# 16 instead of 32 tokens through fetched expert rows, a fixed VectorE order in the last stage, and a tail by column chunks

## The chip, the cores and the metric

One core of one Trainium2 chip runs the kernel. The metric is the device time of one execution in microseconds (us), the median of the runs. A profiled execution gives, beside its time, a trace of the instructions of each engine: TensorE (PE for matmuls, PEld for weight loads), VectorE (DVE), ScalarE (ACT), GpSimd (POOL) and the DMA queues of SyncE (SP), ScalarE and GpSimd.

## The reference

A decoder block on x of 256 tokens by 1024 features, all float32. First an RMSNorm, one input projection, two attention mixers of 8 heads each, gates, output projections and a residual add. Then the part that takes most of the time, an expert retrieval (PEER):

```python
qh = (x_blk @ w_q).reshape(tc, PEER_HEADS, 2, PEER_HALF)
scores = jnp.einsum('thpc,hpnc->thpn', qh, skf)           # 8 heads, 2 halves, 128 sub-keys
s_top, i_top = lax.top_k(scores, PEER_TOPK)               # 16 best of each half
cand = s_top[:, :, 0, :, None] + s_top[:, :, 1, None, :]  # 256 candidates
c_s, c_pos = lax.top_k(cand.reshape(...), PEER_TOPK)      # 16 experts per head
g = jax.nn.softmax(c_s, axis=-1)
u = expert_u[e_idx]; v = expert_v[e_idx]                  # rows out of 16384 experts
a = jax.nn.gelu(jnp.einsum('td,thkd->thk', x_blk, u), approximate=False)
out = jnp.einsum('thk,thkd->td', g * a, v)
```

The result is added to the residual and goes through a last RMSNorm.

## The kernel before, in words

The front (to about 253 us) does norms, projections and attention. What follows computes the experts densely for most tokens: the 16384 experts are 128 chunks of 128 (NB = 128).

**Stage U** (lines 628 to 690). For each chunk b a 512 KB block of expert_u is fetched by SyncE (L85, four buffers "raw"), split by ScalarE into a rounded high part whi (L106) and by VectorE or GpSimd into the rest wlo (L109), and multiplied with the tokens in 24 matmuls (mm3, L122: 16 with whi, then 8 with wlo), each on ND columns. ND is T - S = 256 - S; S = 32 tokens are left out of the dense work, so ND = 224. ScalarE takes GELU of the result into W[:, b] (L646). The buffers of whi and wlo are two each, so whi of chunk b waits until TensorE is through with whi of chunk b - 2. VectorE's instructions of the stage run in the order in which they are written (manual_schedule). Between the chunks stand steps of the top-k search, taken from a generator: each step yields a cost in us, and at each chunk the loop adds a rate to what is allowed: EARLY_RATE 2.4 until the first 128 tokens (tt = 1) are done, TOPK_RATE 1.1 after. While the early rate holds, GpSimd makes wlo; the switch comes when `scattered` is filled.

At the end of tt = 1 the gates gS and the places iS are known (L565 to L567), and GpSimd scatters the gates into a zeroed DRAM array gd with 128 indirect DMAs (L487); the 16 of a head must have landed before those of the next but one may write. For the other tile (tt = 0) the S tokens' indices and gates go to DRAM, and for the rest, P - S = 96 tokens, the gates are built into W on the chip in groups of four tokens (24 groups, g_build and g_use, L590 to L622), spread over the chunks that are left.

The program as a whole is ordered by a scheduler that runs a timeline of its own: on engines without a fixed order an instruction is placed when its inputs are ready there and the engine is free, wherever it is written; `issue_after` ties an instruction behind another one.

**Stage V** (L800 to L817). For each chunk b: fetch and split a block of expert_v, weigh two chunks of W with the gates read back from gd (fetch_weights L695 on GpSimd's queue, weigh L702), split W[:, b] into two parts xw (prepare: L707 on ScalarE, L709 on VectorE; xw has two buffers), and 16 matmuls into 8 accumulators: order 0 with v high on both parts (L720, 2 x ND = 448 columns) and order 1 with v low (L723, ND = 224 columns). The first fetch_weights waits for all of the scatter.

The 32 left-out tokens go by fetched rows: S // 16 = 2 groups, in each 16 gathers of expert_u rows and 16 of expert_v rows (L738 on GpSimd's queue, 128 rows of 4 KB each, two buffers), each followed by one VectorE instruction on 128 x 1024 (L749 dot product with the token, L761 weighted sum), 64 in all; at the end of a group 8 matmuls (L765). VectorE's order here is the scheduler's, with these instructions and xw tied behind the newest wlo.

**Tail.** The last LAST = 3 chunks are multiplied column chunk by column chunk c; as each of the 8 is complete, gather_up adds its three parts (L774, L775), finish transposes it (L783), adds it to h (L784) and takes squares for the norm on ScalarE (L786). Then the norm's scale (L828 to L835, with Ln and Exp on ScalarE) and four output pieces. The table for Ln and Exp is asked for at L755.

## Time and profile before

| | us |
|---|---|
| median of three runs | 1022.54 |
| lowest, highest | 1016.17, 1027.51 |
| the profiled execution | 1021.67 |
| its span, first to last instruction | 1019.9 |
| PE busy in the span | 952.3 |
| DVE busy | 767.4 |
| ACT busy | 564.0 |
| POOL busy | 430.4 |

The span is what the trace shows; the time is 1.8 us longer. Matmuls overlap and their ends are modelled, so a busy PE is read by how far apart matmuls start, not by its share. In rows with a line (L122) the line is that of the kernel before; in brackets stands the idle time of the engine before the instruction and what ended it.

### The profile page before, as it was taken

What the parts mean: (1) busy time and instruction counts of PE and PEld (TensorE: products, weight loads), DVE (VectorE), ACT (ScalarE), POOL (GpSimd) and SP (SyncE); (2) the same over time, 40 slices, a digit from 0 to 9 for tenths busy, and PEclk for the clock granted to TensorE, in tenths of its full rate; (3) what the DMA queues carried; (4) which work ended last, traced back from release to release, by engine and by line L of the source; (5) the groups of instructions that cost most, each with busy time, mean ns of one, the idle gap of its engine ahead of it and who ended that gap; (6) DMA issues with size and microseconds to landing.
All of it is one profiled execution on the core that took longest, in us unless ns stands there. A gap on an engine that the chain in (4) does not pass through costs nothing. (4 is left out here: it accounts for less than half of the span.)

```text
span 1019.9 us, 18735 instructions
## 1 busy us (share of the span) xinstructions
PE 952.3 (93%) x7099; PEld 903.6 (89%) x7099; DVE 767.4 (75%) x1433; ACT 564.0 (55%) x1032; POOL 430.4 (42%) x288
## 2 busy tenths in 40 slices
PE   9999999999888999999999998798998998889894
PEld 7898899799888999999999998787987888888793
DVE  6556767764899997777888886788788777778763
ACT  5564446543654567777777674444544444444445
POOL 0000000000657787787787783344444344444201
PEclk9999999999999999999999999999999999999997
DMA  7667685545456879777778677898988888988841
GB/s 238 211 211 247 192 255 179 181 143 167 153 148 168 203 192 237 178 190 197 176 187 199 172 195 235 322 324 302 353 311 303 287 304 291 307 281 305 279 158 42
DMA packets 86298, 230.16 MB, mean 226 GB/s; under 512 B 27392, under 2 KB 30272, under 8 KB 86080
## 3 DMA queue, kind: packets, MB, share of 16 engines
q1 hardware_dynamic: 53216, 183.07, 56.4%
q0 software_dynamic: 31008, 43.07, 15.9%
q10 hardware_dynamic: 1984, 2.84, 0.9%
q8 instruction: 55, 0.90, 0.3%
q14 instruction: 35, 0.29, 0.1%
HBM read 218.35 MB, written 10.58 MB: 224 GB/s over the span
## 5 line engine op out<-in xcount | busy, mean ns | idle before, releaser
L106 ACT CAST whi<-raw 128x1024 fp32r<-128x1024 f32 x327 | 343.5, 1050 | 379.7 <-PE acc L720 186.5
L109 DVE TENSOR_TENSOR wlo<-raw,whi 128x1024 fp32r<-128x1024 f32 x313 | 382.0, 1221 | 115.2 <-ACT whi L106 108.9
L122 PE MATMUL pj<-xh,whi 128*128 128x224 f32 (+1 forms) x1280 | 304.5, 279 | 5.8 <-ACT whi L106 5.8
L122 PE MATMUL pj<-xl,whi 128*128 128x224 f32 (+1 forms) x1280 | 303.8, 279 | 0.1
L720 PE MATMUL acc<-xw,whi 128*128 128x448 f32 x1024 | 237.7, 372 | 39.1 <-DVE xw L709 38.3
L487 POOL DMA_INDIRECT gd<-gS,iS x128 | 242.8, 1897 | 70.8 <-issue 35.8
L122 PEld LDWEIGHTS pj<-xh,whi 128*128 128x128 f32 x1280 | 248.2, 194 | 6.9 <-ACT whi L106 6.2
L122 PEld LDWEIGHTS pj<-xl,whi 128*128 128x128 f32 x1280 | 248.1, 194 | 0.6 <-DVE xl L182 0.4
L720 PEld LDWEIGHTS acc<-xw,whi 128*128 128x128 f32 x1024 | 182.9, 188 | 60.7 <-DVE xw L709 45.1
L122 PE MATMUL pj<-xh,wlo 128*128 128x224 f32 (+1 forms) x1280 | 175.8, 279 | 3.7 <-DVE wlo L109 3.7
L122 PEld LDWEIGHTS pj<-xh,wlo 128*128 128x128 f32 x1280 | 159.8, 193 | 5.1 <-DVE wlo L109 3.9
L109 POOL TENSOR_TENSOR wlo<-raw,whi 128x1024 fp32r<-128x1024 f32 x14 | 33.5, 2408 | 267.1 <-ACT whi L106 260.3
L723 PEld LDWEIGHTS acc<-xw,wlo 128*128 128x128 f32 x1024 | 135.4, 191 | 3.5
L723 PE MATMUL acc<-xw,wlo 128*128 128x224 f32 x1024 | 137.5, 273 | 0.0
L695 POOL DMA_DIRECT2D gq<-gd x64 | 37.0, 579 | 110.0 <-DVE W L702 57.6
L738 POOL DMA_INDIRECT rows<-in_v_dram,places x32 | 57.8, 1805 | 52.7 <-DVE sm L761 36.9
L738 POOL DMA_INDIRECT rows<-in_ur_dram,places x32 | 53.7, 1678 | 49.7 <-DVE rows L749 47.6
L707 ACT CAST xw<-W 128x224 fp32r<-128x224 f32 x128 | 47.5, 373 | 3.6 <-DVE W L702 3.4
L709 DVE TENSOR_TENSOR xw<-W,xw 128x224 fp32r<-128x224 f32 x128 | 49.3, 386 | 0.2
L749 DVE SCALAR_TENSOR_TENSOR rows<-rows,xr 128x1024 f32<-128x1024 f32 x32 | 39.0, 1221 | 10.1 <-DMA rows<-in_ur_dram,places 8.1
L646 ACT ACTIVATE W<-pj 128x224 f32<-128x224 f32 (+24 forms) x128 | 41.5, 324 | 8.4 <-PE pj L122 8.4
L761 DVE SCALAR_TENSOR_TENSOR sm<-rows,a,sm 128x1024 f32<-128x1024 f32 x30 | 38.4, 1280 | 0.4 <-DMA rows<-in_v_dram,places 0.3
(212 smaller groups left out, 967.2 us busy)
## 6 DMA issues: line engine op xcount, KB each, us to landing
raw<-in_ut_dram SPq DMA_DIRECT2D x128, 512.0 KB, 4.0
raw<-in_v_dram SPq DMA_DIRECT2D x128, 512.0 KB, 4.2
raw<-in_wf_dram SPq DMA_DIRECT2D x72, 512.0 KB, 3.9
gd<-zfill SPq DMA_DIRECT2D x16, 512.0 KB, 5.1
gq<-gd POOLq DMA_DIRECT2D x64, 128.0 KB, 4.7
gd<-gS,iS POOLq DMA_INDIRECT x128, 5.0
h<-in_x_dram SPq DMA_DIRECT2D x4, 256.0 KB, 4.8
sks<-in_skt_dram ACTq DMA_DIRECT2D x1, 1024.0 KB
```

Source lines behind the costliest of these rows:

```text
L106: last_hi = nc.scalar.copy(hi, src)
L109: last_lo = rest.tensor_sub(lo, src, hi.bitcast(F32))
L122: nc.tensor.matmul(o, a, b, start=first and i == 0, stop=last and i == len(seq) - 1)
L487: d = nc.gpsimd.indirect_dma_start(gd[:, :], bass.IndirectOffsetOnAxis(ap=iS[:, k:k + 1], axis=0), gS[:, k:k + 1], None, compute_op=ALU.add)
L646: gl = nc.scalar.activation(W[:, b, nd:ND], ps[:, nd:ND], AF.Gelu)
L707: nc.scalar.copy(w[:, 0], W[:, b])
L709: nc.vector.tensor_sub(w[:, 1], W[:, b], w[:, 0].bitcast(F32))
L720: nc.tensor.matmul(acc[c][:, S:S + 2 * ND], v_h[:, cs], w.rearrange("p a b -> p (a b)"), start=b == 0, stop=False, skip_group_check=True)
L723: nc.tensor.matmul(acc[c][:, S:S + ND], v_l[:, cs], w[:, 0], start=False, stop=b == NB - 1, skip_group_check=True)
L738: nc.gpsimd.indirect_dma_start(rows[n][:, :], None, (u_rows if kind == "u" else v_rows)[:, :], bass.IndirectOffsetOnAxis(ap=places[:, g, k ...
L749: nc.vector.scalar_tensor_tensor(r, r, 1.0, xr, op0=ALU.mult, op1=ALU.mult, accum_out=a[:, g, k:k + 1])
L761: nc.vector.scalar_tensor_tensor(sm, r, a[:, g, k:k + 1], sm, op0=ALU.mult, op1=ALU.add)
```

## The change

- S goes from 32 to 16: ND is 240, one group of fetched rows (32 gathers and VectorE products, not 64), 28 groups of gates built on the chip, not 24.
- The top-k generator: its costs and TOPK_RATE are raised; all four index casts of ScalarE are written after the first pair of the second search; Exp and the normalisation are written later; GpSimd hands wlo back to VectorE when the searches of tt = 1 end (`shared`), not when the scatter is issued.
- Stage V: VectorE in the written order (wlo, xw of the next chunk, weigh, then a fetched row's product at most once in two chunks); xw has three buffers; ScalarE's half of xw is tied behind whi.
- The table load for the norm is tied behind the last GELU.
- Tail: LAST is 2; PE, VectorE and ScalarE in the written order; squares of columns 0 to 511, 512 to 895 and the last 128 are taken in three pieces, half on VectorE; the product with the norm's gains on GpSimd comes before the norm's scale is known.

```diff
-LAST = 3
+LAST = 2
-TOPK_RATE = 1.1
+TOPK_RATE = 1.3
-S = 32
+S = 16
-    xsp = ctx.enter_context(tc.tile_pool(name="xsplit", bufs=2))
+    xsp = ctx.enter_context(tc.tile_pool(name="xsplit", bufs=3))
+            shared = ["searches"]
                         yield from best16([(sv[:, pp, k16], si[:, pp, k16], sc[tt][:, 2 * hd + pp])
-                                           for pp in range(2)], 0.205)
+                                           for pp in range(2)], 0.25)
...
-                        pp, hh = h0 // 4, 4 * (h0 // 2 % 2)
-                        nc.scalar.copy(sx[pp][:, hh:hh + 4]...)
-                        yield from best16([...], 0.14)
+                        if h0 == 2:
+                            for pp in range(2):
+                                for hh in (0, 4):
+                                    nc.scalar.copy(sx[pp][:, hh:hh + 4]...)
+                                yield 0.0
+                        yield from best16([...], 0.2)
+                    shared.clear()
+                    yield 0.0
...
-                    nc.scalar.activation(ge, ge, AF.Exp)
...
+                        if pp == 0:
+                            nc.scalar.activation(ge, ge, AF.Exp)
...
-                        nxt = load(ut[b + 1], [P, 8, P], rest=nc.vector if scattered else nc.gpsimd)
+                        nxt = load(ut[b + 1], [P, 8, P], rest=nc.gpsimd if shared else nc.vector)
...
-                        allowed += TOPK_RATE if scattered else EARLY_RATE
+                        allowed += EARLY_RATE if shared else TOPK_RATE
...
         def prepare(b):
             w = (vp if b == NB - 1 else xsp).tile([P, 2, ND], F32R, name="xw", tag="xw")
-            nc.scalar.copy(w[:, 0], W[:, b])
-            with tc.issue_after(last_lo.ins):
-                nc.vector.tensor_sub(w[:, 1], W[:, b], w[:, 0].bitcast(F32))
+            with tc.issue_after(last_hi.ins):
+                nc.scalar.copy(w[:, 0], W[:, b])
+            nc.vector.tensor_sub(w[:, 1], W[:, b], w[:, 0].bitcast(F32))
...
                         if g == ng - 1:
-                            nc.scalar.preload_act_table_set("natural_log_exp_and_others")
+                            with tc.issue_after(gl.ins):
+                                nc.scalar.preload_act_table_set("natural_log_exp_and_others")
...
+        with tc.manual_schedule(engines={mybir.EngineType.DVE}):
+            for b in range(NB):
+                v_h, v_l = load(v[b], [P, D], vp if b % 3 == (NB - 1) % 3 else splp)
+                if b == 0:
+                    weigh(0)
+                    w_next = prepare(0)
+                parts = (v_h, v_l, w_next)
+                if b + 1 < NB:
+                    w_next = prepare(b + 1)
+                if b % 2 == 0:
+                    weigh(b + 2)
+                    fetch_weights(b + 4)
...
+                if b % 2 and b >= 3:
+                    while done * (NB - 24) <= (b - 3) * 32 * ng:
+                        next(steps, None)
+                        done += 1
...
+        with tc.manual_schedule(engines={mybir.EngineType.PE, mybir.EngineType.DVE, mybir.EngineType.Activation}):
+            for c in range(4):
+                for order in range(2):
+                    products(b0, c, parts0, order)
+            for c in range(8):
+                for order in range(2):
+                    products(b1, c, parts1, order)
+                    if c < 4:
+                        products(b0, c + 4, parts0, order)
+                rests.append(gather_up(c))
+                if c:
+                    finish(c - 1, rests[c - 1])
+                if c == 5:
+                    squares_of(0, 0, 4)
+                    for tt in range(2):
+                        nc.gpsimd.tensor_mul(h[:, tt, :512], h[:, tt, :512], gf[:, :512])
+            squares_of(1, 4, 7)
+            finish(7, rests[7])
+            squares_of(2, 7, 8)
```

## Rows read from the trace of the kernel before

**Rows 1.** The head of the page.
```profile
span 1019.9 us, 18735 instructions
```

**Rows 2.** Busy time by stretches of the span: the stretch, its length, then busy us and instructions of PE, PEld, DVE, ACT, POOL, the granted clock, the DMA share, GB/s.
```profile
253.10:308.50 55.40, 48.25 (x399) 47.70 (x397) 49.71 (x227) 29.30 (x41) 33.51 (x14) 0.94 0.48 147
...
387.00:623.40 236.40, 236.40 (x2114) 236.40 (x2112) 186.79 (x259) 172.91 (x416) 181.93 (x98) 1.00 0.78 193
626.60:645.00 18.40, 16.09 (x96) 14.59 (x96) 10.82 (x17) 8.55 (x14) 4.87 (x10) 1.00 0.95 336
645.00:977.00 332.00, 298.22 (x1826) 276.01 (x1825) 260.95 (x380) 151.73 (x230) 142.47 (x119) 1.00 0.87 301
```

**Rows 3.** Matmuls of TensorE in order of time (start us, us, line): the first and the last of 16 that follow one another on 256 columns, and of 16 on 224 columns.
```profile
230.18 0.28 PE L122 MATMUL pj<-uh,whi 128*128 128x256 f32 x1
...
231.96 0.28 PE L122 MATMUL pj<-ul,whi 128*128 128x256 f32 x1
...
598.38 0.28 PE L122 MATMUL pj<-xh,whi 128*128 128x224 f32 x1
...
600.06 0.27 PE L122 MATMUL pj<-xl,whi 128*128 128x224 f32 x1
```

**Rows 4.** The chain of work that ended last, in stage V (start us, us until the next piece, what).
```profile
961.40 1.91 PE acc L720 x8
...
966.00 1.19 DVE sm L761
967.55 1.91 PE acc L720 x8
...
975.37 1.70 PE acc L765 x16
...
982.20 1.63 PE acc L720 x8
983.83 0.88 PE acc L723 x8
```

**Rows 5.** One row of the view of waits: who waited, for whom, us in all, times, longest.
```profile
PE acc L720 <- DVE xw L709: 38.3, 48, 3.0
```

**Rows 6.** Groups of VectorE's instructions by line over the whole span (line, operation, out<-in, shapes, count | busy us, mean ns | idle before).
```profile
L109 DVE TENSOR_TENSOR wlo<-raw,whi 128x1024 fp32r<-128x1024 f32 x313 | 382.0, 1221 | 115.2 <-ACT whi L106 108.9 <-PE pj L241 2.4 <-PE pj L122 2.1
L709 DVE TENSOR_TENSOR xw<-W,xw 128x224 fp32r<-128x224 f32 x128 | 49.3, 386 | 0.2
L749 DVE SCALAR_TENSOR_TENSOR rows<-rows,xr 128x1024 f32<-128x1024 f32 x32 | 39.0, 1221 | 10.1 <-DMA rows<-in_ur_dram,places 8.1 <-DMA xr<-xd 2.0
L702 DVE TENSOR_TENSOR W<-W,gq 128x256 f32<-128x256 f32 x64 | 26.8, 419 | 4.4 <-DMA gq<-gd 4.4
```

**Rows 7.** From the scatter to stage V, in order of time: VectorE's places iS, GpSimd's first scatter and the first read of gd, TensorE's first product of V.
```profile
307.92 0.29 DVE L567 TENSOR_SCALAR iS<-W,pcol 128x128 uint32<-128x128 f32 x1
308.50 1.79 POOL L487 DMA_INDIRECT gd<-gS,iS  x1 [6.11 <-DVE W L472]
619.88 1.17 POOL L695 DMA_DIRECT2D gq<-gd  x2 [3.94 <-DMA gd<-gS,iS]
626.62 1.65 PE L720 MATMUL acc<-xw,whi 128*128 128x448 f32 x7 [3.02 <-DVE xw L709]
```

**Rows 8.** The three gaps of TensorE early in stage U, and ScalarE's instructions at two of them; the first row is ScalarE's at the start of the kernel.
```profile
2.03 1.28 ACT L755 ACT_TABLE_LOAD   x1
269.68 1.99 ACT L528 CAST W<-W 128x1024 bf16<-128x1024 uint32 x2 [4.90 <-DVE W L474]
272.91 0.37 PE L122 MATMUL pj<-xh,whi 128*128 128x224 f32 x1 [3.02 <-ACT whi L106]
289.79 0.31 ACT L534 ACTIVATE W<-W 128x128 f32<-128x128 f32 x1 [2.71 <-DVE W L533]
292.75 0.37 PE L122 MATMUL pj<-xh,whi 128*128 128x224 f32 x1 [2.77 <-ACT whi L106]
310.82 2.05 PE L122 MATMUL pj<-xh,wlo 128*128 128x224 f32 x8 [3.68 <-DVE wlo L109]
```

**Rows 9.** VectorE in the last steps of tt = 1: the start of the first step after the searches, and the same product twice, the first while GpSimd made a wlo.
```profile
288.89 0.86 DVE L533 TENSOR_TENSOR W<-W 128x128 f32<-128x128 f32 x1
292.81 3.42 DVE L556 TENSOR_TENSOR W<-W 128x2048 bf16<-128x2048 bf16 x1
304.36 1.22 DVE L556 TENSOR_TENSOR W<-W 128x2048 bf16<-128x2048 bf16 x1
```

**Rows 10.** The tail in order of time: the first and the last product, one pair of transposes, the two table loads, the first of the last products on VectorE.
```profile
994.61 0.38 PE L720 MATMUL acc<-xw,whi 128*128 128x448 f32 x1
1002.39 0.35 PE L723 MATMUL acc<-xw,wlo 128*128 128x224 f32 x1
1004.05 0.44 PE L783 MATMUL tpv<-ident,rest 128*128 128x128 f32 x2 [0.56 <-DVE rest L775]
1010.06 1.28 ACT L830 ACT_TABLE_LOAD   x1
1011.58 1.28 ACT L831 ACT_TABLE_LOAD   x1
1013.90 1.41 DVE L843 SCALAR_TENSOR_TENSOR o<-h,st,gf 128x512 f32<-128x512 f32 x2
```

**Rows 11.** DMA issues: out<-in, queue, operation, count, median us from issue to landing.
```profile
rows<-in_ur_dram,places POOLq DMA_INDIRECT x32, 6.3
```

More of the change, by code (lines that the diff above doesn't have):

```diff
@@ L759, in fetched_steps @@
                 else:
-                    with tc.issue_after(last_lo.ins):
-                        nc.vector.scalar_tensor_tensor(sm, r, a[:, g, k:k + 1], sm, op0=ALU.mult, op1=ALU.add)
+                    nc.vector.scalar_tensor_tensor(sm, r, a[:, g, k:k + 1], sm, op0=ALU.mult, op1=ALU.add)
                 yield
@@ L793, in block_kernel @@
         fetch_weights(2)
-        weigh(0)
-        w_next = prepare(0)
-        for b in range(NB):
-            w = w_next
-            parts = (*load(v[b], [P, D], vp if b % 3 == (NB - 1) % 3 else splp), w)
-            if b < NB - LAST:
-                for order in range(2):
-                    for c in (range(8) if b else (4, 5, 6, 7, 0, 1, 2, 3)):
-                        products(b, c, parts, order)
-            else:
-                kept.append((b, parts))
-            if b + 1 < NB:
-                w_next = prepare(b + 1)
-            if b % 2 == 0:
-                weigh(b + 2)
-                fetch_weights(b + 4)
-            if b == 3:
-                nc.scalar.dma_start(gf, gf_row.partition_broadcast(P))
-                nc.scalar.dma_start(sel, consts[:, 1153:1153 + GS])
-            if b >= 1:
-                while done * (NB - 12) <= (b - 1) * 64:
-                    next(steps, None)
-                    done += 1
@@ L817, in block_kernel @@
-        rests = []
-        for c in range(8):
-            for b, parts in kept:
-                for order in range(2):
-                    products(b, c, parts, order)
-            rests.append(gather_up(c))
-            if c > 1:
-                finish(c - 2, rests[c - 2])
-        finish(6, rests[6])
-        finish(7, rests[7])
-        ss, r, t = st[:, 20:22], st[:, 22:24], st[:, 24:26]
-        nc.vector.tensor_reduce(ss, sq, AX.X, ALU.add)
-        nc.vector.tensor_scalar(ss, ss, 1.0 / D, EPS, op0=ALU.mult, op1=ALU.add)
@@ L830, in block_kernel @@
[L830 to L844 removed]
+        with tc.manual_schedule(engines={mybir.EngineType.DVE}):
[10 more added lines that the diff above has]
+                    fetch_weights(b + 4)
+                if b == 3:
+                    nc.scalar.dma_start(gf, gf_row.partition_broadcast(P))
+                    nc.scalar.dma_start(sel, consts[:, 1153:1153 + GS])
+                if b < NB - LAST:
+                    for order in range(2):
+                        for c in (range(8) if b else (4, 5, 6, 7, 0, 1, 2, 3)):
+                            products(b, c, parts, order)
+                else:
+                    kept.append((b, parts))
+                if b % 2 and b >= 3:
+                    while done * (NB - 24) <= (b - 3) * 32 * ng:
+                        next(steps, None)
+                        done += 1
@@ new lines, in block_kernel @@
+        rests = []
+        ss, r, t = st[:, 20:22], st[:, 22:24], st[:, 24:26]
+        (b0, parts0), (b1, parts1) = kept
+        with tc.manual_schedule(engines={mybir.EngineType.PE, mybir.EngineType.DVE, mybir.EngineType.Activation}):
+            for c in range(4):
+                for order in range(2):
+                    products(b0, c, parts0, order)
+            for c in range(8):
+                for order in range(2):
+                    products(b1, c, parts1, order)
[11 more added lines that the diff above has]
+            squares_of(2, 7, 8)
+            nc.vector.tensor_reduce(ss, sq, AX.X, ALU.add)
+            nc.vector.tensor_scalar(ss, ss, 1.0 / D, EPS, op0=ALU.mult, op1=ALU.add)
+            nc.scalar.activation(r, ss, AF.Ln)
+            nc.scalar.activation(r, r, AF.Exp, scale=-0.5)
+            nc.vector.tensor_mul(t, r, r)
+            nc.vector.tensor_mul(t, t, ss)
+            nc.vector.tensor_scalar(t, t, -0.5, 1.5, op0=ALU.mult, op1=ALU.add)
+            nc.vector.tensor_mul(r, r, t)
+            for tt in range(2):
+                o = rawp.tile([P, D], F32, name="o", tag="raw")
+                rt = r[:, tt:tt + 1]
+                nc.scalar.activation(o[:, :512], h[:, tt, :512], AF.Copy, scale=rt)
+                nc.vector.scalar_tensor_tensor(o[:, 512:], h[:, tt, 512:], rt, gf[:, 512:], op0=ALU.mult, op1=ALU.mult)
+                nc.scalar.dma_start(out[tt][:, :512], o[:, :512])
+                nc.sync.dma_start(out[tt][:, 512:], o[:, 512:])
```

59 lines of the change are left out of this document (23 added, 36 removed).

## The prediction

> **What bounds the kernel now.** I read the stretches first, then the order of time at their seams, the chain of waits, and the groups of instructions.
>
> The span is 1019.9 us [rows 1]. The front, to 253.1, is the same code before and after, so I keep it. Stage U lasts to 623.3. From 387 on TensorE is without a gap: 2114 matmuls in 236.4 us, 0.112 us each; at its start it is not: 399 in 55.4 us, at a granted clock of 0.94 [rows 2]. Three gaps stand there, 3.02, 2.77 and 3.68 us [rows 8]. 128 chunks of 24 matmuls at 0.1115 us are 342.5 us, the 24 groups 24 x 4 x 0.119 = 11.4; 370.2 us passed, so U loses 16.3.
>
> The first product of V stands at 626.62, and what released it is not the end of U. VectorE makes iS at 307.92, the first scatter goes at 308.50, and the first read of gd goes at 619.88, ended by the scatter's landing [rows 7]. From iS to V's first product 318.7 us pass on GpSimd's queue, whatever TensorE does meanwhile. U ended 3 us earlier by coincidence.
>
> In V a chunk that waits for nothing takes 1.63 + 0.88 = 2.51 us; where a fetched row's product stands in the chain, two chunks take 6.15 us (961.40 to 967.55) instead of 5.02 [rows 4]. TensorE waited 38.3 us for xw [rows 5]. VectorE has, per chunk, wlo 1.22, xw 0.39, half of a weighing 0.21, and 64 fetched products of 1.22 to 1.28 over 116 chunks, 0.69: together 2.51, all of a chunk [rows 6]. With two xw buffers, xw of the next chunk starts only when TensorE is through with the last one, and any long instruction ahead of it becomes a gap. Loss in all: the last three chunks start at 994.61 [rows 10]; with one of them counted in, 126 chunks took 997.1 - 626.6 = 370.5 us, against 316.3 + 3.4 for the two groups' small matmuls, so V loses 50.8 us.
>
> **The change part by part.**
>
> *Columns.* ND = 240 is 7% more for TensorE, but that isn't what the spacing says. 16 columns take 1.70/16 = 0.106 us each, 224 columns 0.110 in V [rows 4] and 0.112 in U (15 steps in 1.68 us), 256 columns 0.1187 [rows 3], 448 columns 0.2038. Below some 235 columns something other than columns sets the spacing; above, the line from 256 to 448 has 0.000443 us per column. It gives 0.1116 at 240 and 0.2180 at 480. I take 0.1125 for 240, just over the floor; bounds are 0.110 and 0.1153 (halfway between 224 and 256). The cost in U is 24 x 0.001 x 128 = 3.1 us (bounds -5 to 12); four more groups are 1.9. A chunk of V becomes 8 x (0.2180 + 0.1125) = 2.644 us, so 126 chunks are 333.1 instead of 316.3: +16.8 (+14 to +20).
>
> The Trainium skill, "TensorE: Matmul & The Clock Gate", section "Back-to-back issue gap", gives a gap of N/2.4 + 2.5 ns; by it alone each 240-column matmul costs 6.7 ns more than a 224-column one. The same page's "LDWEIGHTS" has a weight load at columns/1.2, 107 ns for 128, which is the floor that the 16-column matmuls show. The sum goes by the floor; a price in columns is rival 2.
>
> *Top-k and the scatter.* The searches of tt = 1 are the same instructions and end at 288.89 [rows 9]. From there to iS took 19.0 us. In it four instructions were stretched while GpSimd made a wlo: L556 took 3.42 beside it and 1.22 alone [rows 9]; with three short ones that were held in the same way (the first, L533, took 0.86) the excess adds up to 7.1, so the steps alone are 12. After the change GpSimd makes no wlo in this stretch, but VectorE makes those of chunks 14 to 21: by the new costs the searches end in chunk 12 (29.0 at 2.4 each) and iS comes in chunk 20 (12.5 more at 1.3). 288.9 + 12 + 8 x 1.13 = 310.0. TensorE can be later: wlo of chunk 21 waits for whi, that for chunk 19's high products, 253.1 + 19 x 2.70 + 1.8 = 306.2, then 1.05, 1.2 and 0.8: 309.3 plus whatever TensorE has lost by then.
>
> Does it still lose the first two gaps? The change writes ScalarE's casts and Exp later in the program. But ScalarE isn't in written order here: a table load written in V (L755) ran at 2.03, and the casts that waited 4.90 us ran four chunks before the chunk that they were written in [rows 8]. Their inputs don't change, so I lean to the gaps staying. They cost 3.02 + 2.77 and about 3.3 of half clock behind them (matmuls 0.21 apart), 9.1. So iS is at 310.0 to 318.4, and V starts 318.7 later, at 628.7 to 637.1; I take the middle, 633 (+6.4). The third gap, wlo queued behind steps on VectorE, goes, since the steps are now handed out 1.3 us a chunk. But U's end no longer matters: 253.1 + 345.6 + 13.3 + some 7 is 619, and TensorE then idles some 14 us for the scatter.
>
> VectorE in the group part of U becomes fuller: 28 groups of about 3.3 us over 75 chunks, 93 + 75 x 1.31 = 191 of 216 us, where it had 187 of 236 [rows 2]. ScalarE's waits inside a group could then reach TensorE; up to 9 us of that is hidden by the idle time before V. The cover fails at 11.
>
> A fuller VectorE could also slow the scatters. They take 1.55 at best and 1.88 on average while VectorE is 79% busy; if the excess went with its busy time, 128 x 0.33 x 0.13 = 6 us. The Trainium skill, "SBUF — State Buffer", section "Who interferes with whom", says that GpSimd can't write descriptors while VectorE holds the shared ports in its two-port modes, which products of two tensors don't have. By that rule the added work, all such products, costs the scatters nothing. No run here separates the two; 0 stands in the sum and 6 in the range.
>
> *Stage V.* VectorE has 1.22 + 0.41 + 0.21 + 32 x 1.25 over 104 chunks, 0.38: 2.22 of 2.644 us. xw is written ahead of the fetched product, and with a third buffer it may be made two chunks ahead, so a 1.25 us instruction behind it has more than a chunk of cover. ScalarE's half of xw goes behind whi, one chunk earlier than needed. A gather is asked for two steps, over six chunks or 16 us, before its product; it lands in 6.3 us [rows 11]. What stays is the start: six chunks in 18.4 us [rows 2], 3.3 lost, 1.7 of half clock after the idle time (as behind the gap at 272.91), and 2 for the rest: 7 of the 50.8. Bounds are 3 and 25, half of today's. The DMA share was 0.87 with 0.55 fetched rows (280 KB) per chunk beside 576 KB; with 0.31 rows and a shorter chunk the rate is (576 + 158)/2.644 = 278 GB/s, below the 301 that it ran at [rows 2]. One group's eight small matmuls are 0.9.
>
> *Tail.* From the end of the 126th chunk to the end of the span it was 1019.9 - 997.1 = 22.8. After: 1.3 us for four products of the last but one chunk; then TensorE's written order, in which transposes of c - 1 wait behind products of c for ScalarE's copy and VectorE's add, some 1.2 us after the product. Stepping through the eight, with pairs of transposes of 0.44 [rows 10], the last ends 8.5 later. Then add 0.6, squares of 128 columns 0.5, the scale 1.3 instead of 3.84 since both table loads (1.28 each) go when the load is tied behind the GELU, and 6.0 from the first output product to the end as now [rows 10]: 18.2 (bounds 16.5 to 20.5).
>
> **The sum.** 633 + 333.1 + 0.9 + 7 + 18.2 = 992.2 of span, 27.7 less. The profiled time stands 1.8 above its span, and the median 0.9 above the profiled execution: 995.
>
> **The rivals.**
>
> 1. *VectorE still holds V.* The fixed order makes it stand at one instruction while another is ready, so half of the loss stays, 25 us. For it: 84% busy leaves little. Against: the third buffer. 995 + 18 = 1013.
> 2. *Columns cost in proportion.* 0.1195 for 240. U: 367 + 13.3 + 9 puts its end at 642.6, past the scatter; V starts at 646 and its chunk is 2.69: 646 + 338.9 + 0.9 + 7 + 18.6 + 2.7 = 1014. Against it are 16 to 224 columns at one spacing [rows 3, 4].
> 3. *The group part of U is VectorE's.* If its end slips by over 11 us, V starts then, not at the scatter; with 20 it is 1004.
> 4. *A fetched row blocks wlo (slower).* In fixed order a product whose row hasn't landed holds every wlo behind it. If GpSimd's queue, where gathers stand behind reads of gd, sends a gather only after the last product, it costs 1.8 + 6.3 less 3.5 of cover, 4.6 us, 32 times: 147, so 1140. It decides from 0.9 us a row (28 us over 32). For it: VectorE waited 8.1 us for rows [rows 6]. Against: two buffers.
> 5. *ScalarE's steps don't move.* That is one end of the forecast (637), not apart from it.
>
> **How the numbers follow.** Forecast 0.72, rival 1 0.13, rival 2 0.06, rival 3 0.05, rival 4 0.04. A measurement of this kernel tells about 1% from no change, that is 1012 to 1033. The forecast's low end: V from 628.7, 3 lost, tail 17, and scatters 4 shorter, 980; its high end with V from 640 and 15 lost, 1010. With part of rival 1 the range is 980 to 1012. Faster by over 1%: 0.72 + 0.05 + about 0.08 of rivals 1 and 2, and low outcomes of them, 0.87; within 1%: 0.08; slower 0.05.
>
> **What would show it.** Right: matmuls of 240 columns 0.112 to 0.114 apart; the first scatter at 310 to 319 and V's first product some 318 behind iS with TensorE idle ahead of it; chunks of V near 2.64 with hardly a wait for xw; no table load at L830's place. Wrong: U's end releasing V, a chunk of V at 2.7 or more, or VectorE waiting for rows.

## The result and the profile after

The kernel after takes 989.0 us (984.65 to 990.61), the kernel before 1019.95 beside it: a ratio of 0.968, 95% interval 0.961 to 0.975. The forecast was 995, in a range of 980 to 1012. The profiled execution after is 988.83 us with a span of 987.1, so 32.8 us less of span than before. Three stretches in order of time say where they went:

| | before | after | difference |
|---|---|---|---|
| first product of V | 626.62 | 632.11 | +5.5 |
| the 126 chunks from there | 370.5 | 335.3 | -35.2 |
| from there to the end of the span | 22.8 | 19.7 | -3.1 |

The page and the stretches of the kernel after, with the columns of [rows 2]:

```profile
span 987.1 us, 18618 instructions
```
```profile
254.40:310.00 55.60, 51.59 (x440) 51.01 (x439) 42.38 (x220) 33.16 (x46) 31.02 (x13) 0.97 0.57 166
...
400.00:628.50 228.50, 224.60 (x1953) 221.25 (x1951) 193.01 (x267) 176.98 (x426) 178.58 (x98) 1.00 0.73 178
632.10:650.00 17.90, 17.38 (x87) 15.38 (x88) 10.40 (x17) 7.76 (x12) 6.40 (x10) 0.86 0.71 254
650.00:940.00 290.00, 290.00 (x1777) 265.49 (x1777) 222.47 (x325) 150.68 (x224) 78.46 (x84) 1.00 0.84 282
```

From 650 to 940 TensorE is busy in all of 290 us, where before it stood 33.8 of 332 us still [rows 2]; VectorE is busy in 222. The 38.3 us of waiting for xw [rows 5] are gone but for one wait, the one of 4.3 us at V's start. VectorE's waits for ScalarE's half of xw between 650 and 940, and its groups over the span (columns as in [rows 5] and [rows 6]):

```profile
DVE xw L717 <- ACT xw L716: 66.5, 77, 2.9
```
```profile
L109 DVE TENSOR_TENSOR wlo<-raw,whi 128x1024 fp32r<-128x1024 f32 x314 | 382.6, 1220 | 39.3 <-ACT whi L106 23.9 <-PE pj L122 9.4 <-PE pj L241 2.4
L717 DVE TENSOR_TENSOR xw<-W,xw 128x240 fp32r<-128x240 f32 x128 | 52.0, 407 | 78.2 <-ACT xw L716 78.0
L756 DVE SCALAR_TENSOR_TENSOR rows<-rows,xr 128x1024 f32<-128x1024 f32 x16 | 19.5, 1220 | 4.1 <-DMA xr<-xd 4.1
```

These 66.5 us of VectorE's (78.0 over all of V) cost nothing: TensorE has no idle time between 650 and 940. The one wait for data is xr at the first fetched product, and no later product waited for its row.

The seam before V in order of time answers to [rows 7]:

```profile
318.45 0.29 DVE L576 TENSOR_SCALAR iS<-W,pcol 128x128 uint32<-128x128 f32 x1
319.03 1.79 POOL L487 DMA_INDIRECT gd<-gS,iS  x1 [21.06 <-DVE W L472]
...
621.05 2.15 POOL L487 DMA_INDIRECT gd<-gS,iS  x1 [0.30 <-issue]
626.68 1.16 PE L122 MATMUL pj<-xh,wlo 128*128 128x240 f32 x8 [0.72 <-DVE wlo L109]
626.94 1.17 POOL L704 DMA_DIRECT2D gq<-gd  x2 [3.75 <-DMA gd<-gS,iS]
630.67 0.43 DVE L710 TENSOR_TENSOR W<-W,gq 128x256 f32<-128x256 f32 x1 [2.73 <-DMA gq<-gd]
632.11 3.54 PE L728 MATMUL acc<-xw,whi 128*128 128x480 f32 x8 [4.27 <-DVE xw L717]
```

The scatter still releases V: in the page's chain that ended last, GpSimd's L487 has 22% of the span. But U's last matmul ends only 4.3 us ahead, at 627.8. And at the gaps of [rows 8]:

```profile
268.27 2.00 ACT L532 CAST W<-W 128x1024 bf16<-128x1024 uint32 x2 [2.20 <-DVE W L474]
277.62 2.00 ACT L532 CAST W<-W 128x1024 bf16<-128x1024 uint32 x2 [2.58 <-DVE W L474]
...
288.18 0.31 ACT L562 ACTIVATE W<-W 128x128 f32<-128x128 f32 x1 [2.50 <-DVE W L541]
```
```profile
280.87 0.38 PE L122 MATMUL pj<-xh,whi 128*128 128x240 f32 x1 [0.92 <-ACT whi L106]
291.16 0.39 PE L122 MATMUL pj<-xh,whi 128*128 128x240 f32 x1 [2.77 <-ACT whi L106]
```

ScalarE's casts and Exp still run as soon as the scheduler sees room, not where the program now writes them, and a whi stands behind each. The third gap, a wlo behind steps, is gone.

The tail ([rows 10] before) has no table load between the squares and the scale:

```profile
974.96 0.44 PE L790 MATMUL tpv<-ident,rest 128*128 128x128 f32 x2
...
975.16 0.69 DVE L798 SCALAR_TENSOR_TENSOR sqo<-h 128x512 f32<-128x512 f32 x1
...
975.20 2.99 POOL L850 TENSOR_TENSOR h<-h,gf 128x512 f32<-128x512 f32 x2 [0.51 <-ACT sqo L797]
...
977.21 1.40 DVE L798 SCALAR_TENSOR_TENSOR sqo<-h 128x384 f32<-128x384 f32 x1
...
978.54 0.41 DVE L791 TENSOR_TENSOR h<-h,tpv 128x256 f32<-128x256 f32 x1
...
979.88 0.20 ACT L856 ACTIVATE st<-st 128x2 f32<-128x2 f32 x1 [0.43 <-DVE st L855]
...
981.14 1.42 DVE L866 SCALAR_TENSOR_TENSOR o<-h,st,gf 128x512 f32<-128x512 f32 x2
```

### The profile page after: what moved, and what is told of

Its sections match the earlier page's. It is cut to its first block, busy times and chain, and to the rows that moved or that the text cites. A ratio compares the mean times of both kernels' runs of the same rounds, so it can differ in the third digit from the quotient of the medians.

```text
span 987.1 us, 18618 instructions
## 1 busy us (share of the span) xinstructions
PE 959.3 (97%) x7099; PEld 902.7 (91%) x7099; DVE 742.0 (75%) x1399; ACT 572.1 (58%) x1021; POOL 363.9 (37%) x254
## 4 chain that ended last, share of the span: by engine, by line
PE 35%; POOL 22%; DMA 6%; issue 5%; DVE 2%; ACT 0%; POOLq 0%; ACTq 0%; DVEq 0%
POOL gd L487 22%; PE acc L728 21%; PE acc L731 11%; DMA gd<-gS,iS 5%; PE pj L122 2%; DMA xr<-xd 1%; DVE wlo L109 0%; DMA gq<-gd 0%; DVE rest L782 0%; PE acc L772 0%; DVE sqo L798 0%; ACT o L865 0%; POOL rows L746 0%; DVE W L565 0%; DVE rows L756 0%
## 5 line engine op out<-in xcount | busy, mean ns | idle before, releaser
L122 PE MATMUL pj<-xh,whi 128*128 128x240 f32 (+1 forms) x1280 | 303.1, 279 | 5.3 <-ACT whi L106 5.3
L122 PE MATMUL pj<-xl,whi 128*128 128x240 f32 (+1 forms) x1280 | 301.0, 277 | 0.1
L487 POOL DMA_INDIRECT gd<-gS,iS x128 | 239.9, 1874 | 85.3 <-issue 36.9
L728 PE MATMUL acc<-xw,whi 128*128 128x480 f32 x1024 | 245.6, 381 | 4.3 <-DVE xw L717 4.3
L122 PE MATMUL pj<-xh,wlo 128*128 128x240 f32 (+1 forms) x1280 | 175.7, 279 | 1.9 <-DVE wlo L109 1.6
L731 PE MATMUL acc<-xw,wlo 128*128 128x240 f32 x1024 | 137.7, 275 | 0.5 <-DVE wlo L109 0.5
L717 DVE TENSOR_TENSOR xw<-W,xw 128x240 fp32r<-128x240 f32 x128 | 52.0, 407 | 78.2 <-ACT xw L716 78.0
L655 ACT ACTIVATE W<-pj 128x240 f32<-128x240 f32 (+24 forms) x128 | 43.3, 338 | 25.3 <-PE pj L122 19.6
L716 ACT CAST xw<-W 128x240 fp32r<-128x240 f32 x128 | 49.4, 387 | 7.9 <-DVE W L710 6.9
L746 POOL DMA_INDIRECT rows<-in_v_dram,places x16 | 26.1, 1634 | 43.0 <-DVE sm L768 37.0
L608 ACT ACTIVATE JR<-iota,njT 128x128 fp32r<-128x128 f32 x112 | 36.0, 396 | 0.0
```

The lines of the kernel that those rows point to most:

```text
L122: nc.tensor.matmul(o, a, b, start=first and i == 0, stop=last and i == len(seq) - 1)
L487: d = nc.gpsimd.indirect_dma_start(gd[:, :], bass.IndirectOffsetOnAxis(ap=iS[:, k:k + 1], axis=0), gS[:, k:k + 1], None, compute_op=ALU.add)
L608: nc.scalar.activation(JR[:, q], iota, AF.Abs, bias=njT[:, t:t + 1])
L655: gl = nc.scalar.activation(W[:, b, nd:ND], ps[:, nd:ND], AF.Gelu)
L716: nc.scalar.copy(w[:, 0], W[:, b])
L717: nc.vector.tensor_sub(w[:, 1], W[:, b], w[:, 0].bitcast(F32))
```

## The experiments

The change bundles five edits that can bear on V and its ends. The time of V is compared below by its first 125 chunks, so that two or three kept chunks make no difference. They took 368.0 us before and 332.6 after; without any loss they would take 125 x 2.51 = 314 with 32 tokens and 125 x 2.612 = 326.5 with 16. The theory at the outset: VectorE's order, the third buffer and the fewer products each carry a part. The kernel before was run beside each group of experiments; its medians lie between 1018.3 and 1022.3 us, so times of two experiments that differ by less than some 4 us are told apart by their traces only.

**32 tokens in the new kernel.**
```
-S = 16
+S = 32
```


> The kernel after, but with 32 tokens fetched again (S = 32): the new order of VectorE, the third buffer of xw and the new tail stay. A chunk of V is then 24 matmuls of 224 and 448 columns, 2.51 us; VectorE has 1.22 + 0.41 + 0.21 + 64 x 1.25 / 104 = 2.61 us of work in each, more than a chunk. Theory (the order takes most of the loss, the tokens are needed so that VectorE fits): V is VectorE's, 104 x 2.61 + 22 x 2.51 = 327 us and some 10 of loss, about the 335 of the kernel after, so 982 to 995 in all, and TensorE waits for xw or wlo in V by some 10 to 15 us. Rival 1 (the order alone does it, VectorE has room): V is 316.3 + 6 = 322, 973 to 978 in all. Rival 2 (the tokens alone do it): V loses some 45 us again, 362 us, 1010 to 1016.

(A slip in it: a chunk of V is 16 matmuls, eight of each width.) 1014.4 us, ratio to before 0.994 (0.991 to 0.997); 125 chunks took 361.0. By its time rival 2 holds, yet for a reason that none of the three had: VectorE's work is not what fills the chunk, it stands for rows. VectorE's waits between 650 and 940 with TensorE's behind them, and one such place in order of time:

```profile
DVE sm L768 <- DMA rows<-in_v_dram,places: 26.2, 13, 4.2
DVE xw L717 <- ACT xw L716: 18.3, 20, 2.1
DVE rows L756 <- DMA rows<-in_ur_dram,places: 11.3, 6, 2.5
...
PE acc L731 <- DVE wlo L109: 23.9, 10, 3.6
```
```profile
661.87 1.04 PE L731 MATMUL acc<-xw,wlo 128*128 128x224 f32 x8
...
668.25 1.22 DVE L756 SCALAR_TENSOR_TENSOR rows<-rows,xr 128x1024 f32<-128x1024 f32 x1 [2.50 <-DMA rows<-in_ur_dram,places]
...
669.41 1.22 DVE L109 TENSOR_TENSOR wlo<-raw,whi 128x1024 fp32r<-128x1024 f32 x1
...
670.68 2.00 PE L731 MATMUL acc<-xw,wlo 128*128 128x224 f32 x8 [3.61 <-DVE wlo L109]
```

This is the mechanism of the prediction's rival 4: a row that has not landed holds the wlo written behind its product, and TensorE with it.

**16 tokens in the old kernel.**
```
-S = 32
+S = 16
-                while done * (NB - 12) <= (b - 1) * 64:
+                while done * (NB - 12) <= (b - 1) * 32 * ng:
```


> The kernel before, but with 16 tokens fetched (S = 16): VectorE's instructions of V in the scheduler's order, two buffers of xw, the old tail, the old top-k pace. A chunk of V is 2.61 us. Theory (order and buffer needed): each of 32 fetched products still costs what each of 64 cost before, 50.8/64 = 0.79 us, so V loses 25 and is 329 + 25 = 354 us; with V's start near 632 and a tail of 22.8 the time is 1008 to 1014. Rival 2 (the tokens alone do it): V loses 6 to 10, 338 us, 992 to 997.

1017.9 us, ratio 0.997 (0.994 to 1.0005): no change that can be told, and slower than the theory's 1008 to 1014. 125 chunks took 362.2, 5.8 less than before, though 12.5 of columns came on top; some 36 of them are loss, where the theory had 25. Halving the tokens takes the rows' waits and some of those for xw away, but with two buffers TensorE still waits for xw: 15.7 us, 29 times, between 650 and 960, against 29.8 and 42 before. The tokens alone are worth nothing.

**Two buffers of xw in the new kernel.**
```
-    xsp = ctx.enter_context(tc.tile_pool(name="xsplit", bufs=3))
+    xsp = ctx.enter_context(tc.tile_pool(name="xsplit", bufs=2))
```


> The kernel after, but with two buffers of xw instead of three. Theory (the third buffer is what hides a fetched product of 1.25 us): TensorE waits for xw again by 0.3 to 0.6 us at each of 32 products, 10 to 20 us, so 999 to 1009. Rival (the written order with the product last is enough, since VectorE has 0.4 us a chunk to spare): under 3 us, 988 to 992.

1018.35 us, ratio 0.995 (0.993 to 0.998): without this one buffer next to nothing of the gain is left, a worse outcome than the theory's 999 to 1009. 125 chunks took 353.6, 21.0 more, a little over the theory's 20. The waits between 650 and 930: TensorE's in this kernel (the kernel after has none there), ScalarE's in this kernel, and then ScalarE's in the kernel after:

```profile
PE acc L728 <- DVE xw L717: 8.1, 12, 1.7
PE acc L731 <- DVE wlo L109: 2.8, 10, 0.3
```
```profile
ACT whi L106 <- DMA raw<-in_v_dram: 102.9, 60, 3.3
```
```profile
ACT whi L106 <- PE acc L728: 77.7, 63, 1.5
...
ACT whi L106 <- DMA raw<-in_v_dram: 10.6, 6, 2.6
```

With two buffers xw of chunk b + 1 can be made only when TensorE is through with chunk b - 1. In VectorE's order every wlo stands behind xw, so it frees its raw buffer later, and the transfer of the next weights starts later; ScalarE then waits for raw 102.9 us instead of 10.6. With three, ScalarE waits for TensorE instead. This chain is read from the program's order and the waits; no run takes it apart. TensorE pays at two places of a chunk: over the 125 chunks, the time from a chunk's last matmul to the next chunk's first grew by 10.9 us in all, and that from the last with whi to the first with wlo by 4.5. The rest of the 21.0 is spread: 480-column matmuls stand 0.220 us apart in the median instead of 0.214, for a reason that stays open.

The other 9.9 us of this profiled execution lie ahead of V, which starts at 642.01: iS came at 322.92, and its scatter took 307.4 us from first to last issue instead of 302.0. The order of instructions in U is the same in both, and in three other kernels here with that order iS comes 64.2 to 64.4 us behind U's first matmul, in the kernel after 64.1, in this one 68.1. So this part is not explained by the edit; it stays open, and what the third buffer is shown to be worth here is the 21.0 us in V.

**VectorE's order left to the scheduler in the new kernel.** The four operations of V are tied behind last_lo as before and the fixed order is dropped for VectorE:
```
-        with tc.manual_schedule(engines={mybir.EngineType.DVE}):
+        if True:
...
+            with tc.issue_after(last_lo.ins):
                 nc.vector.tensor_sub(w[:, 1], W[:, b], w[:, 0].bitcast(F32))
```


> The kernel after, but VectorE's instructions of V are ordered by the scheduler behind ties to wlo, as in the kernel before; three buffers of xw, 16 tokens and the new tail's order on the other engines stay. Theory (the written order matters beside the buffer): xw lands behind a fetched product or wlo behind it in some of 32 places, 5 to 15 us more, 994 to 1004. Rival (the third buffer and the fewer products do it, the order is nothing): within 2 us of the kernel after.

989.65 us; 125 chunks in 332.1, no wait of TensorE for xw or wlo after 640. The rival holds: the written order, the largest part of the diff, is worth nothing here, with 16 tokens and three buffers of xw.

**ScalarE's casts and Exp where the program has them.**
```
+                                    with tc.issue_after(last_hi.ins):
                                         nc.scalar.copy(sx[pp]...
...
+                            with tc.issue_after(last_hi.ins):
                                 nc.scalar.activation(ge, ge, AF.Exp)
```


> The kernel after, with the four index casts and the Exp on ScalarE tied behind the chunk's whi, so that they run where the program has them. Theory (those two ran early and stood ahead of whi, the gaps of 1.2 and 3.05 us at 280.9 and 291.2 are theirs, and V's start hangs on iS and so on TensorE's pace): both gaps go, with some 1 to 2 us of half clock behind them, iS comes 4 to 6 us earlier (312 to 315), and V starts at 627 to 628.5: 983.5 to 985.5. Rival (the gaps move: VectorE waits for the casts or Exp further on, or U's end, which loses 8 us in its group part, releases V): V's start within 1 us of 632, 988 to 990.

983.4 us (982.76 to 985.75), ratio to before 0.965 (0.961 to 0.969), just below the theory. Its stretch from 254.4 to 310, to be laid beside the row of the kernel after:

```profile
254.40:310.00 55.60, 55.60 (x495) 55.34 (x494) 52.62 (x232) 37.40 (x52) 29.46 (x12) 1.00 0.65 189
```

No gap, the clock at its full level (2.4 GHz) throughout, iS at 309.83, which is the low end that the prediction gave for the case that the steps do move (310.0), and V at 626.34. Both are earlier than expected, in part because U itself began 2.4 us earlier in this execution (251.95 after 254.39; in the fourteen profiled executions it begins between 251.6 and 254.8). Counted from there iS comes 57.9 us behind instead of 64.1, so the edit is worth 6.2 us of iS; the way from iS to V took 2.8 us more, 316.5. Both gaps were ScalarE's, and V's start follows iS.

**Half of the scatters.**
```
-                    for k in range(16 * hd, 16 * hd + 16):
+                    for k in range(16 * hd, 16 * hd + 16, 2):
```


> The kernel after with only every second of the 128 scatters issued (half of the gates of the fetched-weights tokens stay out of gd, so that part of the result is left out). Theory (the chain of scatters from iS releases V, 4 us behind U's end): the first read of gd no longer waits for it, V's first product stands some 1.5 to 3.6 us behind U's last small matmul, 628.5 to 630.5, and 1.5 to 4 us of the time go; VectorE and the matmuls of U are the same. Rival (U's end or VectorE's hand-over at the seam releases V anyway): V's start within 0.5 us of 632.1. If the scatters' memory traffic also slows U's group part, U's loss of 8.4 us in it gets smaller.

V's first product came at 627.98, 1.4 us behind the end of U's last matmul instead of 4.3: the scatter did hold V, by some 3 of the 4.1 us (U itself ended 1.3 earlier here). But the time fell only to 986.9: the 125 chunks took 334.9 instead of 332.6, since TensorE stood 3.6 us in the fifth chunk. TensorE's rows of V's start and of that place, and VectorE's row there:

```profile
627.98 1.98 PE L728 MATMUL acc<-xw,whi 128*128 128x480 f32 x8 [1.44 <-DVE xw L717]
...
644.06 1.86 PE L731 MATMUL acc<-xw,wlo 128*128 128x240 f32 x8 [3.58 <-DVE wlo L109]
```
```profile
641.64 1.22 DVE L756 SCALAR_TENSOR_TENSOR rows<-rows,xr 128x1024 f32<-128x1024 f32 x1 [6.51 <-DMA xr<-xd]
```

In both kernels the load of xr goes out 2.8 us behind V's first product and takes some 10 us. After the shorter idle time the granted clock stayed at 1.00 here, V's first chunk took 2.71 us instead of 5.03 (granted clock 0.50 from 632.1 to 637.0), and the product that needs xr came up sooner. In U's group part the spacings of over 0.3 us exceed the usual 0.112 by 5.0 us in all instead of 5.4, so the scatters' traffic does not cause U's loss there: in this execution the last of the 64 scatters goes out at 479.7, and the loss stays.

**The table load not tied behind GELU.**
```
-                            with tc.issue_after(gl.ins):
-                                nc.scalar.preload_act_table_set("natural_log_exp_and_others")
+                            nc.scalar.preload_act_table_set("natural_log_exp_and_others")
```


> The kernel after, with the load of the table of Ln and Exp not tied behind the last GELU. Theory: the load runs early in V, GELU puts its own table back, and the tail has two table loads of 1.28 us each ahead of Ln and Exp as the kernel before had: 2.6 us more in the tail (22.3 from the end of the 126th chunk), 991 to 992. Rival (one of them hides behind the squares on VectorE, which end last): 1.3 us or less.

990.6 us. Both loads are back, 1.28 us each:

```profile
979.13 1.28 ACT L855 ACT_TABLE_LOAD   x1
980.42 0.20 ACT L855 ACTIVATE st<-st 128x2 f32<-128x2 f32 x1
980.64 1.28 ACT L856 ACT_TABLE_LOAD   x1
```

From the start of the 126th chunk to the end it was 24.47 us instead of 22.32: +2.15 of the 2.57 that the loads take. The theory holds for the tail, with some 0.4 us hidden, and most of the tail's gain is this one tie. The untied load itself ran at 2.03 us, as in the kernel before [rows 8], not early in V.

**48 tokens.**
```
-S = 16
+S = 48
```


> The kernel after with 48 tokens fetched (S = 48): TensorE has 208 and 416 columns. Theory (below some 235 columns the spacing doesn't go by columns): a chunk of U without a gap takes 24 x 0.110 to 0.112 = 2.64 to 2.69 us as with 240 and 224; matmuls of 416 columns are 0.189 apart (the line from 256 to 448). V is VectorE's: 96 products over 104 chunks, 0.92 x 1.25 = 1.15 beside 1.84, 3.0 us a chunk, 375 to 390 us in all, so about 1035 to 1050. Rival (time in proportion to columns): a chunk of U in 24 x 0.097 = 2.33 us, U 45 us shorter.

In U, matmuls of 208 columns start 0.112 us apart in the median, those of 240 columns 0.113: the theory, and no proportion to columns. V was a miss: 453 us for 125 chunks, 1108 in all (one execution), where 375 to 390 were expected. The first two rows are VectorE's waits from 650 to 940, the third TensorE's:

```profile
DVE rows L756 <- DMA rows<-in_ur_dram,places: 43.0, 17, 4.7
DVE sm L768 <- DMA rows<-in_v_dram,places: 41.8, 15, 5.7
...
PE acc L731 <- DVE wlo L109: 69.8, 26, 5.9
```

The expectation counted VectorE's work; what grew was the rows' lateness, as in the run with 32. It was not a longer landing: a row landed in 5.9 us in the median here, against 7.0 to 8.4 there. With two row buffers the gather leaves too late. No run gives 48 tokens a third one.

**Three row buffers with 32 tokens.** The theory by now: 32 tokens do not overfill VectorE; with two row buffers a gather leaves too late. The new kernel with S = 32, and
```
-                    rows[n] = vp.tile([P, D], F32, name="rows", tag="rows", bufs=2)
+                    rows[n] = vp.tile([P, D], F32, name="rows", tag="rows", bufs=3)
...
             gather(0)
+            gather(1)
             for n, (g, kind, k) in enumerate(todo):
-                gather(n + 1)
+                gather(n + 2)
```


> The run with 32 tokens in the new order (1014 us) had VectorE stand 37.5 us for fetched rows in V (26.2 and 11.3, 19 times) and TensorE 23.9 us for wlo behind it: a gather goes out 0.3 us after the product that frees its buffer, two products later it is needed, 6.6 us, and it took 7.1 to 8.4 us to land. This kernel is that one with three row buffers and gathers asked for three products ahead. Theory (the rows' landing is what 32 tokens cost in the written order, not VectorE's work): VectorE's waits for rows fall below 5 us, the first 125 chunks of V take 318 to 328 us instead of 361, and the time is 972 to 982. Rival 1 (VectorE's own work fills the chunk, 2.4 to 2.6 of 2.51 us): the waits go but TensorE waits for wlo or xw by some 10 to 20 us, 125 chunks in 330 to 340, 984 to 994. Rival 2 (the gathers queue for the DMA engines' bandwidth, which is at 0.89 share and 314 GB/s): rows stay late, over 1005.

979.0 us (978.34 to 981.4), ratio 0.958 (0.954 to 0.962). 125 chunks in 330.6 instead of 361.0, a little above the theory's 328; TensorE stands 3.2 us of it behind the wait for xr. VectorE's waits for rows are 0.2 us. Rival 1, whose 330 to 340 the 330.6 just touches, is out by its time and by TensorE's waits for wlo, 3.0 us between 650 and 940. Rival 2 is out too: the DMA share rose to 0.95 and 344 GB/s, and the rows still came in time.

**The same, with ScalarE's steps tied and the products spread.**
```
-                if b % 2 and b >= 3:
-                    while done * (NB - 24) <= (b - 3) * 32 * ng:
+                if b >= 7:
+                    while done * (NB - 18) <= (b - 7) * 32 * ng:
```


> The kernel of 32 tokens with three row buffers, with ScalarE's casts and Exp tied behind whi as in the run of 983.4 us, and with the fetched products spread one at a time over chunks 7 to 115 (before, only in odd chunks from 3 to 107). Theory: the two gaps of U go, iS comes at 308 to 311 and V starts at 619 to 623, its idle time for the scatter some 8 us; the first product no longer waits for xr; V as in the run beside it or 2 to 5 us shorter: 965 to 976. Rival (V stays bound by VectorE or by rows): the time is 5 us below that of the run beside it and no more.

969.1 us (966.36 to 969.25), ratio 0.947 (0.944 to 0.951): the fastest of all. V starts at 621.23 after 8.5 us of idle time for the scatter, 125 chunks take 324.1, 6.4 less than in the kernel above, and the time is 10 us less, twice what the rival allowed. VectorE's first product no longer waits for xr. What each of the two edits gave is not told apart: V starts 5.5 us earlier, and V itself takes 6.4 less.

**The kernel before with a third buffer of xw, and with a third row buffer as well.** The first edit alone, then both; tokens, order, tail and top-k are those of before.
```
-    xsp = ctx.enter_context(tc.tile_pool(name="xsplit", bufs=2))
+    xsp = ctx.enter_context(tc.tile_pool(name="xsplit", bufs=3))
...
-                    rows[n] = vp.tile([P, D], F32, name="rows", tag="rows", bufs=2)
+                    rows[n] = vp.tile([P, D], F32, name="rows", tag="rows", bufs=3)
...
+            gather(1)
...
-                gather(n + 1)
+                gather(n + 2)
```

> The kernel before (32 tokens, the scheduler's order of VectorE, old tail and top-k) with three buffers of xw instead of two, and nothing else. 125 chunks of V took 368.0 us before, 313.8 of it the clean 2.51. Theory (the loop from a chunk's last product over ScalarE's and VectorE's halves of the next xw back to TensorE is what cost, and rows late by a little are waited for in a place where nothing stands behind them): TensorE's waits for xw (29.8 us between 650 and 940) fall below 8, the 125 chunks take 325 to 340, and the time is 978 to 995. Rival 1 (with 32 tokens the rows are late in any order, as in the run of 1014 us): VectorE waits for rows by 25 us or more and the 125 chunks take 350 to 362, 1000 to 1015. Rival 2 (the written order is needed with 32 tokens): TensorE waits for wlo instead of xw by as much, 1012 to 1020.

> The kernel before with three buffers of xw, three row buffers and gathers asked for three products ahead; 32 tokens, the scheduler's order and the old tail and top-k stay. With the written order and the new tail the same buffers took 330.6 us for 125 chunks of V (979 us). Theory (the buffers are all, the written order nothing): 125 chunks in 325 to 335, V's start where it was before (626 to 630), a tail 3 us longer: 980 to 988. Rival (the written order counts once VectorE has 2.4 us of work in 2.51): 340 us or more, over 993.

The first: 995.1 us, ratio 0.977 (0.973 to 0.982), 125 chunks in 346.5; TensorE's waits for xw between 650 and 940 fell from 27.4 to 5.1 us (the 29.8 of the expectation are those up to 960). The theory's time came out at its upper edge, V lay above its interval, and rival 1's mark was there too: VectorE waited 27.0 us for rows, and that reached TensorE in one place, where the small matmuls of a finished group stood in its order ahead of a late row's sum:

```profile
PE acc L765 <- DVE sm L761: 11.1, 1, 11.1
PE acc L720 <- DVE xw L709: 5.1, 5, 2.0
```

The second: 972.4 us (970.08 to 975.63), ratio 0.955 (0.950 to 0.959), faster than the theory's 980 to 988. 125 chunks in 321.8, below its 325 to 335, with 32 tokens and the old order. From 650 to 930, and then VectorE's waits up to 940:

```profile
650.00:930.00 280.00, 279.97 (x1784) 266.51 (x1783) 252.97 (x368) 149.30 (x224) 116.35 (x115) 1.00 0.96 348
```
```profile
DVE wlo L109 <- ACT whi L106: 29.6, 51, 2.0
DVE rows L750 <- DMA rows<-in_ur_dram,places: 0.6, 1, 0.6
```

TensorE has no gap while VectorE is busy in 253 of 280 us. A third row buffer beside two buffers of xw was not run.

All of V in one table, 125 chunks. The first two rows and those of 995.1 and 972.4 us are the kernel before with the edit, and the rest is the kernel after with the edit; the two kernels also differ in the tail, in the top-k steps, in ScalarE's half of xw and in how the fetched products are spread. Two rows of the same kernel are a clean comparison; across the two kernels the columns of the table are not all that differs.

| tokens | xw buffers | row buffers | VectorE's order | 125 chunks, us | time, us |
|---|---|---|---|---|---|
| 32 | 2 | 2 | scheduler (before) | 368.0 | 1020 |
| 16 | 2 | 2 | scheduler | 362.2 | 1017.9 |
| 16 | 2 | 2 | written | 353.6 | 1018.4 |
| 16 | 3 | 2 | written (after) | 332.6 | 989.0 |
| 16 | 3 | 2 | scheduler | 332.1 | 989.7 |
| 32 | 3 | 2 | written | 361.0 | 1014.4 |
| 32 | 3 | 2 | scheduler | 346.5 | 995.1 |
| 32 | 3 | 3 | written | 330.6 | 979.0 |
| 32 | 3 | 3 | scheduler | 321.8 | 972.4 |

## Why the prediction was right, step by step

The time, the sign and the three large terms (V's start, the columns, V's loss) came out. U's loss did not, and of the other reasons two were wrong: V's start came out by luck, and V's loss went for another cause than VectorE's work.

*Columns: right.* 240 columns stand 0.112 to 0.113 us apart in U and 0.112 in V, 480 columns 0.214, a chunk of V is 2.612 us for 2.644; over 126 chunks that is 4.0 us less than the sum had. The run with 48 tokens shows the floor at 208 columns too. The prediction's 0.106 for 16 columns is a piece of the chain divided by 16; by their starts those matmuls too stand 0.112 apart, a little above the 107 ns that it set beside them. The Trainium skill, "TensorE: Matmul & The Clock Gate", section "Back-to-back issue gap", gives N/2.4 + 2.5 ns as the gap of an isolated matmul, which would set 208 columns 13 ns below 240; the traces show 1 ns.

*V's start: right in sum (633, measured 632.1), by luck: two errors cancel.* iS came at 318.45, the top of 310.0 to 318.4 instead of the middle taken. The Exp's gap stayed whole and the casts' partly, and VectorE stood 7.8 us, up to 298.31, for a wlo buffer that TensorE had yet to free. That is the prediction's second path, the one by TensorE: its 309.3, with the front's 1.3 us and the 7.1 that U lost in its first thirty chunks, gives 317.7. Against that the chain from iS to V took 313.7 us, not 318.7. The run with tied steps shows the other end of the same forecast.

*U's loss: wrong.* "Some 7" was some 15.5: 7.1 in the first thirty chunks and about 8.4 in the group part, where VectorE is busy in 193 of 228.5 us. The prediction saw the second part coming, called it hidden and left it out of the sum. So TensorE idled 4.3 us before V and not 14, and the cover of 11 for rival 3 was nearly used up. It cost next to nothing because the scatter came later still.

*The scatters beside a fuller VectorE: right at 0.* A scatter took 1.87 us in the mean, 1.90 before.

*V's loss: right in size (7 and 0.9 for the small matmuls; measured 6.1 with them), wrong in its cause.* The small matmuls are 1.7 of it, not 0.9: a group has 16 instructions in the trace, not eight, as the prediction's own 3.4 for two groups says. Of the 4.4 that are left most lies at the start, as forecast: 2.4 us in the first chunk, at half clock, and 0.8 in the fifth, behind the wait for xr, which the prediction did not name. But the reading "VectorE has 2.51, all of a chunk" took a sum of instruction times for a bound. VectorE's instructions overlap: in the kernel with both third buffers their times between 650 and 930 add up to 278 us, and the engine is busy in 253. (In the rows of the run with 32 tokens above, a wlo starts at 669.41, before the product of 668.25 and 1.22 us has ended.) With 32 tokens VectorE does its work there in 90% of the time and TensorE never waits. The trace before told as much: VectorE was busy in 261 of 332 us [rows 2], in which TensorE went through some 114 chunks, and that is 2.29 us a chunk.

What the profile before showed as a wait for xw was look-ahead: one buffer too few. The prediction named that loop and the third buffer, and then gave the same credit to the fewer products and the fixed order. With 16 tokens the order is worth 0. With 32 tokens V takes 9 and 14 us longer in the kernel after, with its written order, than in the kernel before with the same buffers; how much of it is the order, and how much the other differences of the two, no run shows. The worth of halving the tokens hangs on the row buffers. With two, 16 tokens keep the rows in time: 332.6 instead of 361.0 us in the kernel after. With three buffers and the products spread, 32 tokens take 324.1 us of V, and 16 with two buffers 331.8, and U ends at 612.7 and 622.2, in the two kernels with tied steps; 16 tokens with a third row buffer were not run, but their rows are in time without it.

*Rival 4: rightly left aside here, and real.* With 16 tokens a product comes every 8.5 us (104 x 2.612 / 32), with 32 every 4.1. In the run with 32 tokens in the written order a gather left 0.3 us behind the product that freed its buffer, in the place read 6.6 us before the row was needed, and landed in 7.0 (rows of expert_u) to 8.4 us (expert_v) in the median.

*Tail: 18.2 forecast, 19.7 measured.* The table loads went as said. The step that was short is VectorE's: its square of 384 columns took 1.40 us, begun while GpSimd multiplied h by the gains, where 512 columns had taken 0.69, and the last add of h stood behind it, at 978.54. The forecast had no price for GpSimd's product beside it. The scale took some 0.3 us more than its 1.3.

*Front: kept at 253.1, measured 254.4, within the 251.6 to 254.8 of all profiled executions.*

## What to carry to other kernels

A wait for a prepared tile on a nearly full engine looks like an engine that is too slow; before its work is cut, add one buffer to the tile that is waited for, and one to whatever is fetched ahead of it. Here these two edits, four lines, gave 47 us (1019.0 to 972.4), more than the change, and of the change's 31 us 21 are shown to hang on one of the two. Whether an engine is full is read from its busy time, where overlapping instructions count once, not from the sum of their times. An operation that is written later in the program has not moved unless something ties it: look for its start in the trace.

## What the hardware showed that was not expected

- The 128 scatters, the same instructions in each kernel, took 297 to 308 us from the first issue to the last in thirteen profiled executions, and V's start moved with them wherever the scatter released it; what sets their time is open.
- VectorE's squares of h and GpSimd's products of h with the gains held each other up, and the one that began later paid. The square of 512 columns began 0.05 us ahead of GpSimd's first product: it took 0.69 us and the product 1.77, where the second took 1.26 and both took so in the kernel before, which has no such square. The square of 384 columns began during the second product: it took 1.40 us and ended 0.42 behind it. In the nine other kernels with this tail it also ended 0.42 behind it.
- Gathers in V landed in 6.3 us in the median before and in 7.0 to 8.4 with 32 tokens in the new order, at about the same DMA share (0.87 and 0.89); why, stays open. A third row buffer was worth 30.4 us of V in the written order and 24.7 in the old one.
